# Gated-delta sample states as the moving operand in strips of 32 columns, and the convolution tails transposed one stage later

## The chip, the cores and the metric

The kernel runs on one core of a Trainium2 chip. The metric is the device time of one execution in microseconds (us). The engines named below are PE (TensorE, the matrix engine), DVE (VectorE), ACT (ScalarE), POOL (GpSimd) and SP (SyncE, which here only issues DMAs). PEld in a profile is PE's loading of stationary operands.

## The reference, cut to what matters

One inference step of a decoder trunk with four layers: retention, SSD (Mamba-2), gated DeltaNet (GDN below), retention, each followed by a squared-relu MLP. A prompt of 256 rows with empty past and a sample group of 8 sequences with 4 new rows each share the weights, so a matmul moves 288 rows. The change touches the sample group of GDN and the convolution state of SSD and GDN. The core of it, for the one chunk that the sample group has:

```
def step(S, inp):
    u_c, w_c, attn_c, qd_c, kd_c, cd_c = inp
    v_new = u_c - jnp.einsum('bhtk,bhkv->bhtv', w_c, S)
    o_c = jnp.einsum('bthk,bhkv->bthv', qd_c, S) + jnp.einsum('bhts,bhsv->bthv', attn_c, v_new)
    S = S * cd_c[..., None, None] + jnp.einsum('bshk,bhsv->bhkv', kd_c, v_new)
...
o = _rms(o, norm_w) * jax.nn.silu(z ...)
```

For each of 8 sequences b and 16 heads h there is a 128 x 128 state S. The step needs q·S and k·S for 4 rows each: 8 rows of 128 against every one of 128 states. Further, the last 3 rows ahead of each convolution go out as its new state (`new_buf`).

## The kernel before, in words

The dense products (`dense`, L195 to L224) go through PE as three fp32r matmuls for a k tile: ACT casts the weights to a high part (`wh`, L207), DVE takes the rest (`wl`, L210), and L222, L223 and L224 are the three products, each moving 288 columns. All else on PE is plain fp32; such a matmul of the program appears in the trace as two pairs of a weight load and a matmul, so eight in the program are x16 in a row of the trace.

A mixer runs its heads in four units, m = 0 to 3 (`units`). `weave` lets a unit's chain (its preparation, then its loop over chunks of the prompt) advance by one `yield`, and takes fillers for it: the gate's product, parts of the output product, and the projection of the next unit. The number that a chain yields is how much filler it wants (YS for SSD, YG for GDN), and the number of a filler is how much it counts. In GDN a side generator `sample(m)` is interleaved with the projection (`both`). The framework's scheduler then reorders each engine's instructions when the kernel is built, and each engine runs its queue in that order; buffers come from rotating pools, PSUM's small buffers in a pool with tag "m" (3) and tag "s" (2).

In GDN, a unit covers 4 heads. Its preparation makes decays (`ps_dif`), transposes of q and k (`ps_qk`, `ps_qs`), Gram matrices (`ps_gram`), then solves a triangular system: 15 steps on DVE (L1491 and L1492) followed by block products on PE (`ps_W`, `ps_Q`, from L1500 on), and, for the sample group, a small solve of its own (`ps_Y`, L1547 to L1565) that gives `Y2`, `vb2`, `at2` and the row scales `sc2`. The loop then runs over the prompt's chunks (`ps_vn`, `ps_S`, `ps_o`) and normalises (`on`).

`sample(m)` (L1572 to L1612) goes over two pairs of heads. For each head it loads the 8 states (`St`), and for each sequence makes one matmul with the state as the stationary operand and 8 columns of q and k as the moving one (`ps_kS`, 8 in the program for a head). ACT copies the result (`kS`, L1590), two matmuls with the identity transpose it (`ps_u`), DVE and ACT scale it (`r`, L1595; `qo`, L1597), then come `ps_n` with ACT's copy of it (L1601), `ps_o`, DVE's sum `o` (L1605), the square, the mean, POOL's inverse root (`rs_y`) and `on` (L1612), which `ps_oT` transposes for the output product. PSUM tiles of this generator have the tag "s".

`conv_state` (L836 on) transposes the convolution's tail rows (`tl`) through PE (`ps_cs`, PSUM tag "m"), copies them on ACT (`co`, L847) and issues DMAs for them; both mixers call it near the start of a unit's preparation.

Of the kernel before, what the change touches and what calls it, by code (L numbers as in the profile page):

```python
# [35 lines left out]
def make_consts():  # L36
# [87 lines left out]
class K:  # L124
# [808 lines left out]
    def ssd(self, ctx, j, i):  # L933
# [109 lines left out]
        def scan(m):  # L1043
            u = units[m]
            xs, Bt, Ct = u["xs"], u["B"], u["C"]
            hs = slice(8 * m, 8 * m + 8)
            self.conv_state(rp, u["tails"], O["p_ssd_conv"][j], O["s_ssd_conv"][j])

            xdt = rp.tile([128, 2, 512], F32, name="xdt", tag="xdt")
            xw = rp.tile([128, 2, 512], F32, name="xw", tag="xw")  # L1050
# [43 lines left out]
            for g in range(2):  # L1094
                ps = self.ps("ps_g")
                mm(ps[:, 160:416], Bt[g][:, 0:128], Ct[g][:, 0:256])
                mm(ps[:, 0:128], Bt[g][:, 128:256], Ct[g][:, 128:256])
                mm(ps[:, 128:160], rep2[:, 4 + g], Ct[g][:, SEQ:T])
                t = rp.tile([128, 416], F32, name="gm", tag=f"gm{g}")
                V.tensor_tensor(out=t, in0=ps[:, 0:416], in1=gmask, op=ALU.mult)  # L1100
                gm.append(t)
            yield YS[1]

            yi = self.ps("ps_yi")
# [139 lines left out]
    def gdn(self, ctx, j, i):  # L1244
# [109 lines left out]
        T64 = rp.tile([64, 8, 64], F32, name="T64")  # L1354
        G.memset(T64, 0.0)

        def proj(m):
            qk = rp.tile([128, 4, T], F32, name="qk", tag="qk", bufs=2)
            v = [rp.tile([128, T], F32, name="v", tag=f"v{a}") for a in range(4)]
            tails, tl = [], rp.tile([128, 8, 35], F32, name="tl", tag="tl", bufs=2)  # L1360
            for (c0, dst) in ((m * 256, [qk[:, 0], qk[:, 1]]), (1024 + m * 256, [qk[:, 2], qk[:, 3]]), (2048 + m * 512, v)):
                yield from self.conv_dense(rp, xh, xl, w[:, c0:c0 + len(dst) * 128], c0 // 128, rb, cw, cb, None, dst, tails, tl)
            units[m] = {"qk": qk, "v": v, "tails": tails}
# [7 lines left out]
        def prep(m):  # L1371
# [4 lines left out]
            for kh in range(2):  # L1376
                ps = self.ps("ps_dif", "s")
                h0 = 4 * m + 2 * kh
                for r in range(2):
                    mm(ps[:, r * 256:(r + 1) * 256], e2[:, h0 + r:h0 + r + 1].broadcast_to([128, 128]), cts)  # L1380
                Et = rp.tile([128, 2, 2, 128], F32, name="Et", tag=f"Et{kh}")
                pv = ps.rearrange("p (r t y) -> p r t y", r=2, t=2)
                for r in range(2):
                    for tt in range(2):
                        A.activation(Et[:, r, tt], pv[:, r, tt], AF.Abs, bias=nct[:, tt, h0 + r:h0 + r + 1])
                er = rp.tile([128, 2, 128], F32, name="er", tag="er")
                A.activation(er, pv[:, :, 1], AF.Exp)
                e_ = Et.rearrange("p r t y -> p (r t y)")
                A.activation(e_, e_, AF.Exp, scale=-1.0)
                G.tensor_tensor(out=qd[:, 2 * kh:2 * kh + 2], in0=er, in1=bcm(qk[:, kh, 128:256], 2), op=ALU.mult)  # L1390
                Es.append(Et)
            rb2 = rp.tile([128, 32], F32, name="rb2", tag="rb2")
            V.tensor_scalar(out=rb2, in0=i4, scalar1=g2[:, m:m + 1], scalar2=None, op0=ALU.mult)
            ps = self.ps("ps_dif2", "s")
# [2 lines left out]
            V.tensor_scalar(out=e1, in0=ps[:, 0:32], scalar1=gc[:, 32 + m:33 + m], scalar2=None, op0=ALU.subtract)  # L1397
            A.activation(e1, e1, AF.Abs)
            A.activation(e1, e1, AF.Exp, scale=-1.0)
            self.conv_state(rp, u["tails"], O["p_gdn_conv"][j], O["s_gdn_conv"][j], "on", 2)  # L1400

            ssq = rp.tile([128, 10], F32, name="ssq", tag="ssq", bufs=2)
            kt_ = kt("ktok", "vn", 1)
# [145 lines left out]
            def expand(k, t):  # L1549
# [16 lines left out]
            at2 = rp.tile([128, 128], F32, name="at2", tag="at2")  # L1566
            G.tensor_tensor(out=at2.rearrange("p (c y) -> p c y", c=4), in0=bcm(sm[:, 0], 4),
                            in1=b32.rearrange("p (c y) -> p c y", c=4), op=ALU.mult)
            u.update(Tm=Tm, L=L, at=Es, qd=qd, kd=kd, vb=vbs, ncf=ncf, eq=eq, sc2=sc2, Y2=Y2, x4=x4, vb2=vb2, at2=at2)

        def sample(m):
            u = units[m]  # L1572
            while "x4" not in u:
                yield None
            qk, Y2, x4, vb2, at2, sc2, eq = (u[n] for n in ("qk", "Y2", "x4", "vb2", "at2", "sc2", "eq"))
            on2 = u["on2"] = rp.tile([128, 128], F32, name="on2", tag="on2")
            for pr in range(2):
                hp = slice(64 * pr, 64 * pr + 64)

                pT = self.ps("ps_kS", "s")  # L1580
                pv = pT[:, 0:128].rearrange("p (h b c) -> p h b c", h=2, b=DB)
                for h in range(2):
                    St = rp.tile([128, DB, 128], F32, name="St", tag="St", bufs=3)
                    nc.sync.dma_start(St, I["state_gdn"][j, :, 4 * m + 2 * pr + h].rearrange("b k v -> k b v"))
                    for b in range(DB):
                        mm(pv[:, h, b], St[:, b], qk[:, pr:4:2, SEQ + b:T:DB])
                    yield 1.8
                kS = rp.tile([128, 2, 64], F32, name="kS", tag="kS", bufs=2)
                for a in range(2):
                    A.copy(kS[:, a].rearrange("p (h t b) -> p h b t", h=2, b=DB), pv[:, :, :, 4 * a:4 * a + 4])  # L1590
                pu = self.ps("ps_u2", "s")
                for a in range(2):
                    mm(pu[hp, a * 128:(a + 1) * 128], kS[:, a], ident)
                qo, r2, o2 = (rp.tile([128, 128], F32, name=n_, tag=n_) for n_ in ("qo", "r2", "o2"))
                V.scalar_tensor_tensor(out=r2[hp], in0=pu[hp, 128:256], scalar=sc2[hp, 2:3], in1=vb2[hp], op0=ALU.mult,  # L1595
                                       op1=ALU.add)
                A.activation(qo[hp], pu[hp, 0:128], AF.Copy, scale=eg2[hp, m:m + 1])  # L1597
                yield 1.0
                pn = self.ps("ps_n2", "s")
                mm(pn[hp, 0:128], Y2[hp, hp], r2[hp])  # L1600
                A.copy(x4[hp, 1], pn[hp, 0:128])  # L1601
                yield 1.0
                po = self.ps("ps_o2", "s")
                mm(po[hp, 0:128], at2[hp, hp], x4[hp, 1])
                V.tensor_tensor(out=o2[hp], in0=qo[hp], in1=po[hp, 0:128], op=ALU.add)  # L1605
                yield 1.0
                oo = rp.tile([128, 1], F32, name="oo1", tag="oo1", bufs=2)
                A.activation(qo[hp], o2[hp], AF.Square, accum_out=oo[hp])
                ms = rp.tile([128, 1], F32, name="ms1", tag="ms1", bufs=2)
                V.scalar_tensor_tensor(out=ms[hp], in0=oo[hp], scalar=1.0 / 128, in1=eq[hp, 4:5], op0=ALU.mult, op1=ALU.add)  # L1610
                r = self.rsqrt(ms, hp)
                A.activation(on2[hp], o2[hp], AF.Copy, scale=r[hp])  # L1612

        def loop(m):
            u = units[m]
# [212 lines left out]
```

## Time and profile before

| what | us |
| --- | --- |
| median of three runs | 2275.27 (2274.68 to 2281.68) |
| the profiled execution | 2272.98 |
| its span in the trace | 2271.1 |
| PE busy | 2186.3 |
| DVE busy | 1562.4 |
| ACT busy | 1243.3 |
| POOL busy | 580.0 |

The span starts with the first instruction that the trace holds. GDN's mixer stands at about 1060 to 1490 us of it, SSD's at about 520 to 860 us. The units of GDN begin with their first `ps_dif` at about 1122, 1218, 1310 and 1386 us. A row of the timeline gives the start, the duration, the engine and line, the output tile, the operands, and how often the instruction repeats back to back; a bracket at its end is the engine's idle time before it and what ended that.

### The profile page before, as it was taken

The numbers are of one execution on the slowest core, as the hardware profiler recorded it, in microseconds if no ns is written. First come the engines' busy times: TensorE is split into PE (matmuls) and PEld (weight loads), VectorE is DVE, ScalarE is ACT, GpSimd is POOL, SyncE is SP. The second block draws the span as 40 slices with busy tenths as digits, with TensorE's granted clock in tenths as the row PEclk, the third lists the DMA queues.
The fourth block names the chain that finished last, engine by engine and source line by source line (L and its number), as shares of the span: only waits on it lengthen the run. The fifth ranks groups of instructions, "written<-read, shape, count | busy, mean of one in ns | idle before, by whom it ended". The sixth has DMA issues, their size and how long they took to land. (4 is left out here: it accounts for less than half of the span.)

```text
span 2271.1 us, 43130 instructions
## 1 busy us (share of the span) xinstructions
PE 2186.3 (96%) x16332; PEld 2019.0 (89%) x16332; DVE 1562.4 (69%) x3211; ACT 1243.3 (55%) x2827; POOL 580.0 (26%) x605
## 2 busy tenths in 40 slices
PE   9999999998999999999898999989999999999998
PEld 7878899997889889999788987889999878889998
DVE  6777775557888877555886686466766677776554
ACT  4444455554767765545566566366644345445454
POOL 2100113332332222333322122034433001103333
PEclk9999999999999999999899999799999999999999
DMA  7876755545446545545443432257765666664553
GB/s 207 266 255 205 246 186 165 167 153 157 139 146 178 170 128 167 167 150 167 126 133 100 131 120 81 84 156 241 234 204 183 226 231 215 239 232 149 167 167 114
DMA packets 404076, 394.83 MB, mean 174 GB/s; under 512 B 12988, under 2 KB 353573, under 8 KB 403773
## 3 DMA queue, kind: packets, MB, share of 16 engines
q1 hardware_dynamic: 403708, 391.82, 54.3%
q8 instruction: 128, 2.10, 0.4%
q14 instruction: 80, 0.65, 0.1%
q10 hardware_dynamic: 96, 0.20, 0.0%
q0 software_dynamic: 64, 0.07, 0.0%
HBM read 333.36 MB, written 58.69 MB: 173 GB/s over the span
## 5 line engine op out<-in xcount | busy, mean ns | idle before, releaser
L207 ACT CAST wh<-raw 128x512 fp32r<-128x512 f32 x1024 | 627.8, 621 | 687.5 <-PE psd L223 642.5
L210 DVE TENSOR_TENSOR wl<-raw,wh 128x512 fp32r<-128x512 f32 x1024 | 744.3, 734 | 316.3 <-ACT wh L207 292.9
L222 PE MATMUL psd<-xh,wh 128*128 128x288 f32 x2576 | 775.4, 302 | 6.4 <-ACT xh L297 4.6
L224 PE MATMUL psd<-xh,wl 128*128 128x288 f32 x2576 | 771.6, 300 | 4.7 <-DVE wl L210 4.3
L223 PE MATMUL psd<-xl,wh 128*128 128x288 f32 x2576 | 771.0, 300 | 4.0 <-DVE xl L298 3.2
L222 PEld LDWEIGHTS psd<-xh,wh 128*128 128x128 f32 x2576 | 487.1, 189 | 25.1 <-issue 9.6
L223 PEld LDWEIGHTS psd<-xl,wh 128*128 128x128 f32 x2576 | 490.6, 190 | 17.6 <-issue 8.1
L224 PEld LDWEIGHTS psd<-xh,wl 128*128 128x128 f32 x2576 | 489.4, 190 | 13.4 <-DVE wl L210 7.6
L222 PE MATMUL psd<-ah,wh 128*128 128x288 f32 x1536 | 463.5, 302 | 10.0 <-DVE sg L543 3.7
L224 PE MATMUL psd<-ah,wl 128*128 128x288 f32 x1536 | 460.5, 300 | 4.1 <-DVE wl L210 4.0
L223 PE MATMUL psd<-al,wh 128*128 128x288 f32 x1536 | 461.6, 301 | 0.4 <-DVE al L465 0.4
L222 PEld LDWEIGHTS psd<-ah,wh 128*128 128x128 f32 x1536 | 293.9, 192 | 18.9 <-DVE x L442 4.2
L223 PEld LDWEIGHTS psd<-al,wh 128*128 128x128 f32 x1536 | 294.0, 191 | 9.6 <-issue 7.4
L224 PEld LDWEIGHTS psd<-ah,wl 128*128 128x128 f32 x1536 | 294.6, 192 | 7.6 <-DVE wl L210 5.5
L482 POOL TENSOR_TENSOR x<-x,dn 128x288 f32<-128x288 f32 x120 | 149.2, 1243 | 233.2 <-DVE dn L480 233.2
L463 POOL TENSOR_TENSOR a<-v 128x288 f32<-128x288 f32 x128 | 110.2, 861 | 271.9 <-ACT v L462 267.6
L726 DVE SCALAR_TENSOR_TENSOR S<-S,ps_up 128x512 f32<-128x512 f32 x128 | 83.5, 685 | 53.4 <-PE ps_up L725 50.7
L827 DVE SCALAR_TENSOR_TENSOR cacc<-U,cw,cacc 128x312 f32<-128x312 f32 x192 | 106.4, 561 | 8.2 <-ACT cacc L822 5.9
L465 DVE TENSOR_TENSOR al<-a,ah 128x288 fp32r<-128x288 f32 x128 | 59.0, 461 | 67.2 <-POOL a L463 66.5
L263 POOL TENSOR_TENSOR rs_y<-ms,mhalf 128x3 f32<-128x3 f32 (+3 forms) x37 | 36.7, 995 | 237.6 <-DVE ms L742 170.6
L803 POOL COPY U<-cb 128x24 f32<-128x24 f32 x64 | 34.1, 538 | 218.0 <-DVE cacc L827 120.5
L480 DVE TENSOR_TENSOR dn<-psd,rb 128x288 f32<-128x288 f32 x128 | 58.2, 455 | 40.0 <-PE psd L224 40.0
(504 smaller groups left out, 2651.7 us busy)
## 6 DMA issues: line engine op xcount, KB each, us to landing
raw<-mlp_w_up SPq DMA_DIRECT2D x64, 1024.0 KB
raw<-mlp_w_down SPq DMA_DIRECT2D x64, 1024.0 KB
raw<-ret_w_in SPq DMA_DIRECT2D x32, 1024.0 KB
S<-state_ret SPq DMA_DIRECT2D x64, 512.0 KB
s_ret<-S SPq DMA_DIRECT2D x64, 512.0 KB
raw<-ssd_w_in SPq DMA_DIRECT2D x24, 1024.0 KB
raw<-gdn_w_in SPq DMA_DIRECT2D x24, 1024.0 KB
raw<-ret_w_in SPq DMA_DIRECT2D x32, 512.0 KB
```

The source lines that it names most:

```text
L207: self.last_cast = nc.scalar.copy(wh, src)
L210: nc.vector.tensor_tensor(out=wl, in0=src, in1=wh, op=ALU.subtract)
L222: nc.tensor.matmul(po, lhsT=hs[k][:, os], rhs=xh[k], start=(k == 0), stop=False)
L223: nc.tensor.matmul(po, lhsT=hs[k][:, os], rhs=xl[k], start=False, stop=False)
L224: self.last_mm = nc.tensor.matmul(po, lhsT=ls[k][:, os], rhs=xh[k], start=False, stop=(k == kt - 1))
L263: self.nc.gpsimd.tensor_tensor(out=y[rows], in0=ms[rows], in1=self.mhalf[rows].broadcast_to([rows.stop - rows.start, n]), op=ALU.pow)
L463: nc.gpsimd.tensor_tensor(out=a, in0=v, in1=v, op=ALU.mult)
L465: nc.vector.tensor_tensor(out=al[o], in0=a, in1=ah[o], op=ALU.subtract)
L480: nc.vector.tensor_tensor(out=t, in0=ps, in1=rb2, op=ALU.mult)
L482: e.tensor_tensor(out=self.x[o], in0=self.x[o], in1=t, op=ALU.add)
L726: nc.vector.scalar_tensor_tensor(out=S[:, b, z], in0=S[:, b, z], scalar=C["g4"][h], in1=up, op0=ALU.mult, op1=ALU.add)
L827: nc.vector.scalar_tensor_tensor(out=acc[:, 0:n], in0=u, scalar=wk, in1=acc[:, 0:n], op0=ALU.mult, op1=ALU.add)
```

## The change

In `sample`, the states move and the queries and keys are stationary. POOL copies the 4 rows of q and of k of every sequence into a zero-padded tile `Z`, of which a window of 32 columns, chosen by the head, is a stationary operand; sequence b writes the strip of PSUM partitions that starts at 32·(b mod 4). Two sequences and two heads accumulate in a strip, so 16 matmuls, each moving 128 columns, fill one PSUM tile of 128 x 128, and the result is already transposed. The two matmuls of `ps_u` go, one ACT copy stands for two, and DVE's `r` and `o` and ACT's `qo` go. In their place the preparation makes `WQ`: two ACT scalings, two matmuls (`ps_wq`) with a new constant (`gdn_pm`, a permutation, 128 KB) and an ACT copy. `ps_n` and `ps_o` become two accumulating matmuls each. The square and `on` read `ps_o` straight from PSUM. `conv_state` is called after `ps_g` in SSD and after `ps_gram` in GDN. `er` lives in `qd` and has no tile of its own.

```diff
@@ SSD, preparation: the call of conv_state
-            self.conv_state(rp, u["tails"], O["p_ssd_conv"][j], O["s_ssd_conv"][j])
...
                 gm.append(t)
+            self.conv_state(rp, u["tails"], O["p_ssd_conv"][j], O["s_ssd_conv"][j])
             yield YS[1]
@@ GDN, preparation
+        Z = rp.tile([128, 2, DB, 40], F32, name="Z")
+        G.memset(Z, 0.0)
...
+            for pr in range(2):
+                for bh in range(2):
+                    bs = slice(4 * bh, 4 * bh + 4)
+                    G.tensor_copy(Z[:, pr, bs, 8:40].rearrange("p b (a x) -> p b a x", a=2)[:, :, :, bs],
+                                  qk[:, pr:4:2, SEQ:T].rearrange("p a (t b) -> p b a t", b=DB)[:, bs])
...
-            self.conv_state(rp, u["tails"], O["p_gdn_conv"][j], O["s_gdn_conv"][j], "on", 2)
...
                 mm(ps2[cs, 0:64], qk[:, 2 + q // 2, SEQ:T], qk[:, q // 2:4:2, SEQ:T])
+            self.conv_state(rp, u["tails"], O["p_gdn_conv"][j], O["s_gdn_conv"][j], "on", 2)
             yield YG[1]
...
+            t0, t1 = self.t128("wy"), self.t128("wq")
+            A.activation(t0, Y2, AF.Copy, scale=sc2[:, 2:3])
+            A.activation(t1, ident, AF.Copy, scale=eg2[:, m:m + 1])
+            WQ = rp.tile([128, 2, 128], F32, name="WQ", tag="WQ")
+            ps = self.ps("ps_wq", "s")
+            for a, t in enumerate((t0, t1)):
+                mm(ps[:, 128 * a:128 * a + 128], pm[:, a], t)
+            A.copy(WQ.rearrange("p a x -> p (a x)"), ps[:, 0:256])
@@ GDN, sample
                 pT = self.ps("ps_kS", "s")
-                pv = pT[:, 0:128].rearrange("p (h b c) -> p h b c", h=2, b=DB)
                 for h in range(2):
...
                     for b in range(DB):
-                        mm(pv[:, h, b], St[:, b], qk[:, pr:4:2, SEQ + b:T:DB])
-                    yield 1.8
-                kS = rp.tile([128, 2, 64], F32, name="kS", tag="kS", bufs=2)
-                for a in range(2):
-                    A.copy(kS[:, a].rearrange("p (h t b) -> p h b t", h=2, b=DB), pv[:, :, :, 4 * a:4 * a + 4])
-                pu = self.ps("ps_u2", "s")
-                for a in range(2):
-                    mm(pu[hp, a * 128:(a + 1) * 128], kS[:, a], ident)
-                qo, r2, o2 = (rp.tile([128, 128], F32, name=n_, tag=n_) for n_ in ("qo", "r2", "o2"))
-                V.scalar_tensor_tensor(out=r2[hp], in0=pu[hp, 128:256], scalar=sc2[hp, 2:3], in1=vb2[hp], op0=ALU.mult,
-                                       op1=ALU.add)
-                A.activation(qo[hp], pu[hp, 0:128], AF.Copy, scale=eg2[hp, m:m + 1])
+                        c = 32 * (b % 4)
+                        mm(pT[c:c + 32, 0:128], Z[:, pr, b, 8 - 8 * h:40 - 8 * h], St[:, b], h == 0 and b < 4, h == 1 and b > 3)
+                    yield 1.0
+                kS = rp.tile([128, 128], F32, name="kS", tag="kS", bufs=2)
+                A.copy(kS, pT[:, 0:128])
                 yield 1.0
                 pn = self.ps("ps_n2", "s")
-                mm(pn[hp, 0:128], Y2[hp, hp], r2[hp])
+                mm(pn[hp, 0:128], WQ[:, 0, hp], kS, True, False)
+                mm(pn[hp, 0:128], Y2[hp, hp], vb2[hp], False, True)
                 A.copy(x4[hp, 1], pn[hp, 0:128])
                 yield 1.0
                 po = self.ps("ps_o2", "s")
-                mm(po[hp, 0:128], at2[hp, hp], x4[hp, 1])
-                V.tensor_tensor(out=o2[hp], in0=qo[hp], in1=po[hp, 0:128], op=ALU.add)
+                mm(po[hp, 0:128], WQ[:, 1, hp], kS, True, False)
+                mm(po[hp, 0:128], at2[hp, hp], x4[hp, 1], False, True)
                 yield 1.0
...
-                A.activation(qo[hp], o2[hp], AF.Square, accum_out=oo[hp])
+                qo = self.t128("qo")
+                A.activation(qo[hp], po[hp, 0:128], AF.Square, accum_out=oo[hp])
...
-                A.activation(on2[hp], o2[hp], AF.Copy, scale=r[hp])
+                A.activation(on2[hp], po[hp, 0:128], AF.Copy, scale=r[hp])
```

Where the instructions then stand follows from the scheduler. On PE in unit m = 3, the second run of `ps_kS` in the queue of before (`psd` is a dense product, x8 in the program is x16 in the trace):

```order
L222 MATMUL psd<-ah_17880,wh 128x288
L223 MATMUL psd<-al_17884,wh 128x288
L1296 MATMUL ps_o_18703<-lkv,at_18439 64x128
L1296 MATMUL ps_kS<-qk,St 128x8 x16
L224 MATMUL psd<-ah_17880,wl 128x288
L222 MATMUL psd<-ah_17881,wh 128x288
L223 MATMUL psd<-al_17885,wh 128x288
L1296 MATMUL ps_u_18737<-c_ident,kS 64x128
```

And the same place now, up to the first block product of the solve (`ps_W`):

```order
L1302 MATMUL ps_kS<-St,Z 32x128 x15
L227 MATMUL psd<-ah_17874,wh 128x288
L228 MATMUL psd<-al_17878,wh 128x288
L229 MATMUL psd<-ah_17874,wl 128x288
L1302 MATMUL ps_n_18697<-kS,WQ 64x128
L1302 MATMUL ps_n_18697<-vb_18378,Y_18405 64x128
L1302 MATMUL ps_o_18701<-kS,WQ 64x128
L227 MATMUL psd<-ah_17875,wh 128x288
L228 MATMUL psd<-al_17879,wh 128x288
L1302 MATMUL ps_o_18701<-lkv,at_18436 64x128
L1302 MATMUL ps_kS<-St,Z 32x128 x8
L229 MATMUL psd<-ah_17875,wl 128x288
```

Before, both runs of 16 stood between the first `ps_Y` of m = 3 and that `ps_W`, with 96 dense matmuls; now 24 of the 32 stand there, with 70 dense ones, 8 follow behind the first 64 matmuls of `ps_W`, and the second `ps_n` and `ps_o` stand in the block products.

On PE at the start of the preparation of m = 0, before:

```order
L222 MATMUL psd<-xh_14198,wh 128x288 x2
L845 MATMUL ps_cs<-c_ident,tl 35x128 x3
L1296 MATMUL ps_dif<-cts,e_11537 128x256 x2
L223 MATMUL psd<-xl_14199,wh 128x288
L224 MATMUL psd<-xh_14198,wl 128x288
```

and now:

```order
L227 MATMUL psd<-xh_14202,wh 128x288 x2
L1423 MATMUL ps_qk<-c_ident,qk 128x128 x4
L1302 MATMUL ps_dif<-cts,e_11539 128x256 x2
L228 MATMUL psd<-xl_14203,wh 128x288
L229 MATMUL psd<-xh_14202,wl 128x288
```

Transposes of q and k have taken the place of those of the tails, which now follow `ps_gram`. On SP at the end of GDN (`u` and `St` are loads for the states' update that runs beside the MLP, `raw` are weights), before:

```order
L195 DMA raw<-gdn_w_out 128x4x512 x3
L195 DMA raw<-mlp_w_up 128x8x256
L1708 DMA p_gdn<-Sd 128x4x128
L1750 DMA u_19214<-gdn_u 128x256
L1755 DMA St<-state_gdn 128x8x128 x4
L195 DMA raw<-mlp_w_up 128x8x256 x3
```

and now:

```order
L1727 DMA p_gdn<-Sd 128x4x128
L1769 DMA u_19206<-gdn_u 128x256
L1774 DMA St<-state_gdn 128x8x128 x2
L200 DMA raw<-mlp_w_up 128x8x256
L1774 DMA St<-state_gdn 128x8x128 x2
```

The first load of the MLP's weights has moved behind the store of `p_gdn`, the load of `u` and two loads of states.

## Rows read from the trace of the kernel before

**Rows 1.** The page's first part: busy time, share of the span, instructions.

```profile
PE 2186.3 (96%) x16332; PEld 2019.0 (89%) x16332; DVE 1562.4 (69%) x3211; ACT 1243.3 (55%) x2827; POOL 580.0 (26%) x605
```

**Rows 2.** Busy time by stretch, with length, engines' busy time, granted clock, DMA share.

```profile
1130.00:1360.00 230.00, 215.71 (x1988) 199.17 (x1986) 176.00 (x474) 147.38 (x403) 57.39 (x79) 0.99 0.39 119
...
1426.00:1432.00 6.00, 6.00 (x28) 6.00 (x28) 1.62 (x6) 0.65 (x3) 0.00 (x0) 0.50 0.33 89
1434.00:1442.00 8.00, 8.00 (x58) 7.00 (x57) 7.12 (x27) 3.10 (x6) 0.00 (x0) 1.00 0.43 151
1444.00:1456.00 12.00, 12.00 (x46) 9.57 (x46) 4.01 (x12) 1.91 (x7) 0.00 (x0) 0.50 0.01 1
1458.00:1490.00 32.00, 25.93 (x301) 22.79 (x298) 12.38 (x30) 16.59 (x43) 4.93 (x7) 0.91 0.23 75
```

**Rows 3.** PE's timeline in unit m = 0, two groups of ps_kS among dense matmuls.

```profile
1168.49 1.84 PE L1296 MATMUL ps_kS<-qk,St 128*128 128x8 f32 x16
...
1170.40 0.29 PE L223 MATMUL psd<-xl,wh 128*128 128x288 f32 x1
...
1173.45 1.84 PE L1296 MATMUL ps_kS<-qk,St 128*128 128x8 f32 x16
```

**Rows 4.** PE's timeline around ps_qs: 32 stationary columns, 128 moving ones.

```profile
1140.89 0.29 PE L224 MATMUL psd<-xh,wl 128*128 128x288 f32 x1
1141.11 0.65 PE L1296 MATMUL ps_qs<-c_ident,qk 128*32 128x128 f32 x16
...
1141.92 0.29 PE L223 MATMUL psd<-xl,wh 128*128 128x288 f32 x1
```

**Rows 5.** PE's timeline around the two transposing matmuls of the sample group.

```profile
1178.32 0.29 PE L224 MATMUL psd<-xh,wl 128*128 128x288 f32 x1
1178.54 0.65 PE L1296 MATMUL ps_u<-c_ident,kS 128*64 128x128 f32 x4
...
1179.36 0.29 PE L223 MATMUL psd<-xl,wh 128*128 128x288 f32 x1
```

**Rows 6.** PE's timeline in unit m = 3, the two runs of ps_kS.

```profile
1423.60 4.71 PE L1296 MATMUL ps_kS<-qk,St 128*128 128x8 f32 x32
...
1441.20 5.38 PE L1296 MATMUL ps_kS<-qk,St 128*128 128x8 f32 x32
```

**Rows 7.** DVE's timeline in unit m = 3, the solve's steps and its longest waits.

```profile
1422.04 0.16 DVE L1491 TENSOR_TENSOR Ls<-Ls,X 128x15 f32<-128x15 f32 x1
...
1430.37 0.29 DVE L1565 TENSOR_TENSOR Y<-Y,ps_Y 128x128 f32<-128x128 f32 x1 [5.52 <-PE ps_Y L1296]
...
1447.11 0.69 DVE L210 TENSOR_TENSOR wl<-raw,wh 128x512 fp32r<-128x512 f32 x1 [5.22 <-PE psd L224]
...
1449.79 0.36 DVE L1595 SCALAR_TENSOR_TENSOR r<-ps_u,sc,vb 64x128 f32<-64x128 f32 x1 [1.84 <-PE ps_u L1296]
...
1455.03 0.46 DVE L442 TENSOR_TENSOR x<-x,psd 128x288 f32<-128x288 f32 x1 [2.94 <-PE psd L224]
...
1455.86 0.45 DVE L1499 STREAM_TRANSPOSE Ls<-Tm 128x256 f32<-128x256 f32 x1
```

**Rows 8.** PE's waits in GDN's stretch: total us, times, longest.

```profile
PE ps_dif L1296 <- DVE tl L813: 3.5, 1, 3.5
```

**Rows 9.** ACT's timeline at the end of unit m = 0.

```profile
1212.61 0.28 ACT L1590 COPY kS<-ps_kS 128x64 f32<-128x64 f32 x1 [0.77 <-PE ps_kS L1296]
...
1220.28 0.40 ACT L1612 ACTIVATE on<-o,rs_y 64x128 f32<-64x128 f32 x1 [0.77 <-POOL rs_y L263]
```

**Rows 10.** The timeline of all engines at the end of GDN.

```profile
1484.72 0.29 DVE L1605 TENSOR_TENSOR o<-qo,ps_o 64x128 f32<-64x128 f32 x1 [2.57 <-ACT on L1612]
...
1485.05 0.31 ACT L1608 ACTIVATE qo<-o 64x128 f32<-64x128 f32 x1 [0.36 <-DVE o L1605]
```

**Rows 11.** SP's timeline at the end of GDN: issues, with their duration.

```profile
1476.85 0.37 SPq L195 DMA_DIRECT2D raw<-mlp_w_up  x1
...
1490.86 4.17 SPq L1755 DMA_DIRECT2D St<-state_gdn  x4
```

More of the change, by code (lines that the diff above doesn't have):

```diff
@@ L110, in make_consts @@
     c["gdn_m4"] = np.stack([same & (jt[:, None] <= ut[None, :]), same & (ut[None, :] < jt[:, None])], axis=1).astype(f)
+    pm = np.zeros((128, 2, 128), f)
+    for a in range(2):
+        pm[x, a, 32 * (x % 4) + 16 * (1 - a) + 8 * (x // 32 % 2) + 4 * (x % 8 // 4) + x % 32 // 8] = 1.0
+    c["gdn_pm"] = pm
     u1 = np.zeros((128, 2, 128), f)
@@ L1257, in cload @@
             return t
-        b32, lms, gmask, m4, xi0, h16 = (cload(n) for n in ("gdn_b32", "gdn_lms", "gdn_gm", "gdn_m4", "gdn_x0", "gdn_h16"))
+        b32, lms, gmask, m4, xi0, h16, pm = (cload(n) for n in ("gdn_b32", "gdn_lms", "gdn_gm", "gdn_m4", "gdn_x0",
+                                                                "gdn_h16", "gdn_pm"))
         i4, s4 = m4[:, 0], m4[:, 1]
@@ L1385, in prep @@
                         A.activation(Et[:, r, tt], pv[:, r, tt], AF.Abs, bias=nct[:, tt, h0 + r:h0 + r + 1])
-                er = rp.tile([128, 2, 128], F32, name="er", tag="er")
+                er = qd[:, 2 * kh:2 * kh + 2]
                 A.activation(er, pv[:, :, 1], AF.Exp)
@@ L1389, in prep @@
                 A.activation(e_, e_, AF.Exp, scale=-1.0)
-                G.tensor_tensor(out=qd[:, 2 * kh:2 * kh + 2], in0=er, in1=bcm(qk[:, kh, 128:256], 2), op=ALU.mult)
+                G.tensor_tensor(out=er, in0=er, in1=bcm(qk[:, kh, 128:256], 2), op=ALU.mult)
                 Es.append(Et)
+            for pr in range(2):
[3 more added lines that the diff above has]
+                                  qk[:, pr:4:2, SEQ:T].rearrange("p a (t b) -> p b a t", b=DB)[:, bs])
             rb2 = rp.tile([128, 32], F32, name="rb2", tag="rb2")
@@ L1568, in prep @@
                             in1=b32.rearrange("p (c y) -> p c y", c=4), op=ALU.mult)
-            u.update(Tm=Tm, L=L, at=Es, qd=qd, kd=kd, vb=vbs, ncf=ncf, eq=eq, sc2=sc2, Y2=Y2, x4=x4, vb2=vb2, at2=at2)
+            t0, t1 = self.t128("wy"), self.t128("wq")
[6 more added lines that the diff above has]
+            A.copy(WQ.rearrange("p a x -> p (a x)"), ps[:, 0:256])
+            u.update(WQ=WQ, Tm=Tm, L=L, at=Es, qd=qd, kd=kd, vb=vbs, ncf=ncf, eq=eq, sc2=sc2, Y2=Y2, x4=x4, vb2=vb2, at2=at2)
         def sample(m):
@@ L1574, in sample @@
                 yield None
-            qk, Y2, x4, vb2, at2, sc2, eq = (u[n] for n in ("qk", "Y2", "x4", "vb2", "at2", "sc2", "eq"))
+            Y2, x4, vb2, at2, WQ, eq = (u[n] for n in ("Y2", "x4", "vb2", "at2", "WQ", "eq"))
             on2 = u["on2"] = rp.tile([128, 128], F32, name="on2", tag="on2")
```

## The prediction

> **What bounds the kernel now.** I read the shares of busy time first: PE is busy for 96% of the span and DVE for 69% [rows 1], so work taken off PE is worth something wherever DVE does not end the waits. A share over the whole span hides where that is, so the second view is the busy time by stretch, for GDN, the one mixer whose arithmetic changes. From 1130 to 1360 us, units m = 0 to 2 for the most part, PE is busy for 215.7 of 230 us and DVE for 176.0 [rows 2]: PE is the bound, but DVE follows at 77% and ends some of PE's waits. In unit m = 3 it is different. From 1426 to 1432 and from 1444 to 1456 us PE is busy without a gap while its granted clock is 0.50, which is 1.2 in place of 2.4 GHz, and DVE works only 1.6 of 6 and 4.0 of 12 us there [rows 2]. The timeline tells what PE did ahead of each fall: two runs of `ps_kS`, 4.71 and 5.38 us long, with nothing between their matmuls [rows 6]. While they run, the dense products that feed DVE stand behind them in PE's queue: DVE waits 5.52 us for `ps_Y` and 5.22 us for a dense product, and its solve stands still meanwhile [rows 7]. These runs are therefore both work and a block.
>
> **Units m = 0 to 2, by parts.** Between two groups of `ps_kS` 23 dense matmuls start in 1173.45 - 1170.40 = 3.05 us, 0.133 us each [rows 3]. A group (8 in the program, 16 in the trace) takes 1170.40 - 1168.49 = 1.91 us to the second dense start behind it; less one dense matmul that is 1.78 us, about 106 ns for each of the 16 with the change of shape aside [rows 3].
>
> No row shows the new form itself. The nearest is `ps_qs`, which has its very shape, 32 stationary columns in strips and 128 moving columns: from the dense start ahead of it to the second one behind it 1141.92 - 1140.89 = 1.03 us, less two dense matmuls 0.76 us for 16 [rows 4]. The upper bound is that nothing is gained, 1.78 us; the lower one that of `ps_qs`, since no row with that shape is faster. I take 0.76, because shape and operands' type agree, and what differs (it accumulates, and its states come by DMA) changes no count of columns. Twelve groups then save 12 x (1.78 - 0.76) = 12.2 us.
>
> The Trainium skill weighs against this on its page "TensorE: Matmul & The Clock Gate", section "Back-to-back issue gap", which has a sustained pace of about 81 ns per matmul with 128 moving columns and its own weight load. By that, 16 would take 1.30 us and the twelve groups save 5.8 us instead; the row's 0.65 us for 16 speaks against it [rows 4].
>
> The other parts. The two transposing matmuls of a pair of heads cost 1179.36 - 1178.32 - 0.27 = 0.77 us [rows 5] and are gone: 6 x 0.77 = -4.6 us. `ps_n` and `ps_o` have one matmul more each; with the same 0.58 us that the four records of `ps_u` take from 1178.54 on, that is +3.5 us for six pairs. `ps_wq`, two matmuls in a unit, is bounded by nothing and by a `ps_u` apiece; I take 0.77 us, +2.3 us for three units. The scheduler splits some groups among dense work; a change of shape costs 0.76 - 0.58 = 0.18 us, six more of them +1.1 us. The sum is -12.2 - 4.6 + 3.5 + 2.3 + 1.1 = -9.9 us of PE's time.
>
> Not all of it reaches the end, since DVE is busy for 77% and PE already waits 14.3 of 230 us [rows 2]. The same change frees DVE of a little: `r` at 0.36 us [rows 7] and `o` at 0.29 us [rows 10] for six pairs, 3.9 us of 176. I take three quarters, -7.4 us, between -2.5 (DVE ends most waits) and -9.9. ACT loses a copy and `qo` for each pair and gains three operations for each unit, POOL gains four small copies for each unit; neither engine is near its limit here (147.4 and 57.4 of 230 us [rows 2]), so these cost nothing as long as the copies do not stand ahead of an inverse root that is waited for.
>
> **Unit m = 3.** Before, the solve's steps begin at 1422.04 us and its last transpose at 1455.86 us, 33.8 us in all, of which DVE waited 5.52 + 5.22 + 1.84 + 2.94 = 15.5 us in four places [rows 7]. Without these it ends 18.3 us after its start. PE's work up to that point in the new order is 70 dense matmuls (9.3 us), three groups of `ps_kS` (2.3 us) and some ten small matmuls (about 2.5 us by [rows 5]), 14.1 us at the full clock, so DVE would set this stretch and up to 15.5 us would go. Of that something comes back: 30 dense matmuls (4.0 us), one group (0.8 us) and the second `ps_n` and `ps_o` (1.2 us) now stand behind the first `ps_W`, 6.0 us in a stretch where PE idles for 6.1 of 32 us [rows 2] but in a chain that waits for results. I let half of it show, +3 us, and take -12 us. If the clock still falls, 18 us at 0.50 cost 9 us again [rows 2], and only the shorter runs and little more is left, about -4; if all of it works, -15.
>
> **The tails, one stage later.** The count of transposes, copies and DMAs stays. What moves is the wait that PE has for a tail: in GDN 3.50 us once, at a `ps_dif` that stood behind three tail transposes [rows 8]; now transposes of q and k stand there, which need DVE as well, so most of the wait will find another name. I take -1 us, between 0 and -3.5. In SSD no wait of that size is shown and I take nothing, with 2 us to either side. SP's DMAs of the tails move with them, behind loads that nobody waits for.
>
> **The ends.** The last pair's chain loses DVE's `o`, 0.29 us, and the step to the square, 0.36 us [rows 10]: -0.65 us. `ps_o` now keeps its PSUM buffer until `on` has read it; with two buffers of that tag, the next pair's tiles share the other one. The first load of the MLP's weights was issued at 1476.85 us and now goes behind a load at about 1490.5 and two of four that took 4.17 us to issue, thus about 16 us later against the old clock [rows 11]. For both I add 2 us, between 0 and 7.
>
> **The sum.** -7.4 - 12 - 1 - 0.65 + 2 = -19 us. The profiled execution took 2272.98 us, and the median of the runs shown is 2.3 us above it; from the median the forecast is 2275.3 - 19 = 2256 us.
>
> **The rivals.** (A) DVE is the bound. Then units 0 to 2 give 2.5 instead of 7.4 us and m = 3 8 instead of 12: 2256 + 9 = 2265 us. For it speaks DVE's 77%, against it that the long waits in m = 3 are DVE's for PE [rows 7]. (B) The clock falls in m = 3 all the same, since PE then has less work and may stand idle for the solve: +8, 2264 us. Against it: between the two falls, from 1434 to 1442 us, with dense work, the clock was 1.00 [rows 2], and that is what the new order has there. (C) The strips do not overlap, and a group keeps its 1.78 us: three quarters of 12.2 come back, and 4 us in m = 3, 2256 + 13 = 2269 us, which is no change by the bound below. By the skill's pace it would be half of that, 2262 us.
>
> (D) Slower. The sample group's chain from `ps_kS` to `on` becomes what PE waits for. Before it took from 1212.61 to 1220.68 us, 8.1 us, at the end of m = 0 [rows 9], and dense work covered it. The new budgets give it less cover (`yield 1.0` for 1.8, and no `ps_u`), `ps_o` holds one of two PSUM buffers until the chain's end, and the next `ps_dif` needs one of them. If half of the chain, 4 us, lay bare for each of the eight pairs, that is +32, 2288 us; it is slower than before from about 3.3 us for a pair on, since eight of these are the 19 us of the gain and the 7 us of the bound below. Against it: POOL and ACT are half idle, and the same chain shows PE no long wait now. (E) Everything lands: -9.9 and -15 in full, -2 more for the tails, 2256 - 7.5 = 2248 us. That the change does not do what it says is excluded by the order of the instructions.
>
> **How the numbers follow.** The forecast has 0.50 (2250 to 2262), A 0.15, B 0.12, C 0.08, D 0.06, E 0.09. The range reaches from a little below E, which adds gains that no row bounds in SSD, to a little above C: 2246 to 2272 us; D and the tails of the others stay out. About 0.3%, 7 us, is what a measurement of this kernel can tell from no change, so faster means below 2268.4 and slower above 2282.1. Faster are the forecast, E, nearly all of A and B, and half of C: 0.82. Slower is D: 0.06. The rest, 0.12, is the same: half of C, the upper ends of A and B, and a milder D.
>
> **What would show each step right or wrong.** A group of `ps_kS` (x16, form 128*32 128x128) should take 0.65 us in the timeline; at 1.2 or more, C holds. No stretch of m = 3 between its `ps_Y` and its `ps_W` should have a granted clock near 0.50, and DVE should have no wait of 5 us there; the time from the first L1491 step to the last transpose should be near 18 to 22 us, not 33.8. If it is 22 or more with a full clock, DVE set it. PE's waits in GDN for ACT (`on`, `kS`, `x4`) should stay below some 5 us in all; 20 or more means D. The prediction would be wrong in size above all if PE's idle time in units 0 to 2 grows from 14 us by as much as its busy time falls, or if a gap appears in PE at the start of the MLP, where the weights' load now comes later.

## The result and the profile after

The changed kernel takes 2262.31 us in the median of four runs (2258.23 to 2265.39), the kernel before 2278.47 us beside it. The ratio is 0.993 with a 95% interval of 0.990 to 0.996, so it is faster by some 16 us (10 to 23). The forecast was 19. The sum was near, but two of its terms were far off in opposite directions, and the experiments say which.

The page's first part of the kernel after, the line that answers to [rows 1]:

```profile
PE 2175.3 (96%) x16348; PEld 1994.3 (88%) x16348; DVE 1562.1 (69%) x3195; ACT 1242.6 (55%) x2823; POOL 587.5 (26%) x622
```

The shares tell nothing. What tells is the time of a few landmarks on PE in both traces (us; "end" is the last `ps_oT` of GDN):

| | before | after | difference |
| --- | --- | --- | --- |
| first `ps_xt` of SSD | 585.4 | 584.7 | -0.7 |
| first `ps_gc` of GDN | 1112.6 | 1126.3 | +13.7 |
| first `ps_dif` of m = 0 to that of m = 3 | 264.6 | 256.1 | -8.5 |
| first `ps_dif` of m = 3 to the end | 102.3 | 84.7 | -17.5 |
| end to the end of the span | 782.5 | 780.2 | -2.3 |

From SSD's start to GDN's start the kernel after *loses* 14.4 us; GDN then wins 26. A group of `ps_kS` in PE's timeline of the kernel after, to be read against [rows 3] and [rows 4]:

```profile
1184.25 0.29 PE L229 MATMUL psd<-xh,wl 128*128 128x288 f32 x1
1184.47 0.64 PE L1302 MATMUL ps_kS<-St,Z 128*32 128x128 f32 x16
1185.05 0.40 PE L227 MATMUL psd<-xh,wh 128*128 128x288 f32 x1
1185.29 0.29 PE L228 MATMUL psd<-xl,wh 128*128 128x288 f32 x1
```

By the reckoning of the prediction that is 1185.29 - 1184.25 - 0.27 = 0.77 us, where 1.78 stood before. In m = 3, the busy time by stretch of the kernel after (columns as in [rows 2]); the cuts are the first `ps_dif`, the first `ps_Y`, the first `ps_W` behind the solve, and then the clock's fall:

```profile
1391.47:1419.49 28.02, 24.91 (x189) 22.80 (x189) 24.03 (x61) 17.91 (x47) 12.17 (x15) 0.94 0.21 70
1419.49:1434.81 15.32, 15.27 (x138) 12.62 (x136) 13.38 (x45) 6.94 (x17) 0.26 (x1) 1.00 0.48 160
1434.81:1440.00 5.19, 3.76 (x154) 2.88 (x154) 0.80 (x2) 4.04 (x13) 0.78 (x2) 0.94 0.48 173
1440.00:1458.00 18.00, 18.00 (x136) 14.52 (x136) 3.06 (x7) 4.99 (x13) 0.00 (x0) 0.50 0.01 2
1458.00:1477.00 19.00, 17.39 (x129) 16.52 (x128) 8.63 (x22) 9.49 (x22) 4.16 (x5) 0.95 0.21 70
```

and the same three parts before:

```profile
1386.39:1423.49 37.10, 31.81 (x244) 29.29 (x244) 25.85 (x68) 23.27 (x60) 14.65 (x18) 0.95 0.20 68
1423.49:1457.31 33.82, 33.82 (x183) 30.23 (x182) 15.50 (x54) 7.71 (x21) 0.00 (x0) 0.70 0.24 79
1457.31:1488.58 31.27, 25.20 (x356) 22.03 (x355) 11.64 (x28) 16.43 (x43) 4.93 (x7) 0.93 0.24 77
```

From `ps_Y` to `ps_W` 33.8 us became 15.3, at a clock of 1.00 in place of 0.70, with DVE busy for 13.4 of 15.3 us: its long waits are gone. PE is busy for nearly all of these 15.3 us, so DVE alone does not set the stretch. The solve's first step and its last transpose after, on DVE, to be read against [rows 7]:

```profile
1417.31 0.17 DVE L1506 TENSOR_TENSOR Ls<-Ls,X 128x15 f32<-128x15 f32 x1
...
1433.32 0.45 DVE L1514 STREAM_TRANSPOSE Ls<-Tm 128x256 f32<-128x256 f32 x1
```

That is 16.0 us where 33.8 stood before. Behind `ps_W`, up to the last `ps_oT`, 31.3 us became 41.4 with the 18 us at 0.50. The half clock has not gone; it has moved behind the solve. PE's longest waits in GDN after:

```profile
PE psd L229 <- DVE wl L215: 9.2, 6, 2.5
PE ps_Y L1569 <- DVE T L1568: 3.1, 2, 1.7
PE ps_oT L1748 <- ACT on L1703: 2.6, 3, 1.2
PE ps_dif L1302 <- DVE tl L818: 2.5, 1, 2.5
PE ps_S L1302 <- ACT vn L1677: 1.9, 4, 0.6
PE ps_oT L1749 <- ACT on L1631: 1.5, 3, 0.6
```

None of these is a wait for a PSUM buffer that the sample group holds; its `on` (L1631) is waited for as data of `ps_oT`, 1.5 us in all.

The loss in SSD stands in no wait of that size. It is seen in the path from a unit's first `ps_xt` to its first `ps_yi`; in unit m = 3, PE's timeline before:

```profile
805.24 0.60 PE L1054 MATMUL ps_xt<-c_ident,xs 128*128 128x128 f32 x4
...
813.92 0.82 PE L998 MATMUL ps_g<-Ct,Bt 128*128 128x256 f32 x4
...
817.75 0.64 PE L1126 MATMUL ps_yi<-sT,cm 128*32 128x256 f32 x8
```

and after:

```profile
810.78 1.03 PE L1058 MATMUL ps_xt<-c_ident,xs 128*128 128x128 f32 x8
...
819.10 0.59 PE L1003 MATMUL ps_g<-Ct,Bt 128*128 128x256 f32 x2
...
821.51 0.38 PE L850 MATMUL ps_cs<-c_ident,tl 128*35 128x128 f32 x2
824.62 0.84 PE L850 MATMUL ps_cs<-c_ident,tl 128*35 128x128 f32 x6 [1.40 <-ACT co L852]
826.47 0.64 PE L1131 MATMUL ps_yi<-sT,cm 128*32 128x256 f32 x8
```

The path took 12.7, 12.3, 12.3 and 12.5 us in the four units before, and 14.7, 15.8, 16.5 and 15.7 after: 49.8 against 62.7, 12.9 us more.

### The profile page after: what moved, and what is told of

Read it like the earlier page. It is cut to its first block, busy times and chain, and to the rows that moved or that the text cites. A ratio compares the mean times of both kernels' runs of the same rounds, so it can differ in the third digit from the quotient of the medians.

```text
span 2256.4 us, 43194 instructions
## 1 busy us (share of the span) xinstructions
PE 2175.3 (96%) x16348; PEld 1994.3 (88%) x16348; DVE 1562.1 (69%) x3195; ACT 1242.6 (55%) x2823; POOL 587.5 (26%) x622
## 5 line engine op out<-in xcount | busy, mean ns | idle before, releaser
L227 PEld LDWEIGHTS psd<-xh,wh 128*128 128x128 f32 x2576 | 487.2, 189 | 25.6 <-issue 10.1
L227 PEld LDWEIGHTS psd<-ah,wh 128*128 128x128 f32 x1536 | 291.1, 190 | 15.7 <-ACT wh L212 4.9
L832 DVE SCALAR_TENSOR_TENSOR cacc<-U,cw,cacc 128x312 f32<-128x312 f32 x192 | 106.5, 561 | 13.8 <-ACT cacc L827 11.6
```

The costliest lines, as they stand in the source:

```text
L227: nc.tensor.matmul(po, lhsT=hs[k][:, os], rhs=xh[k], start=(k == 0), stop=False)
L832: nc.vector.scalar_tensor_tensor(out=acc[:, 0:n], in0=u, scalar=wk, in1=acc[:, 0:n], op0=ALU.mult, op1=ALU.add)
```

## The experiments

In the tables below, "SSD" is the time from its first `ps_xt` to GDN's first `ps_gc` (527.2 us before, 541.6 after), "m = 3" that from its first `ps_dif` to the end of GDN (102.3 and 84.7). Both are read from one trace of a kernel, the medians from all its runs.

**Which part costs, which gives.** Four kernels, each a call put back or a part alone.

```diff
 # ssd_back: the changed kernel, SSD's call at the start of a unit again
+            self.conv_state(rp, u["tails"], O["p_ssd_conv"][j], O["s_ssd_conv"][j])
             xdt = rp.tile([128, 2, 512], F32, name="xdt", tag="xdt")
...
-            self.conv_state(rp, u["tails"], O["p_ssd_conv"][j], O["s_ssd_conv"][j])
             yield YS[1]
 # gdn_back: the same for GDN's call; sample_only: both; tails_only: the kernel before with both calls late
```

> The changed kernel with one call put back: SSD transposes its convolution tails at the start of a unit, as before. In the two traces the changed kernel reaches GDN 13.7 us later (its first ps_gc at 1126.3 us, against 1112.6), and from there to the last ps_oT it is 26 us shorter. Theory: the call's move in SSD costs 10 to 14 us, since the tails' 4 DMAs a group now stand in SP's queue ahead of the loads of SSD's states. Then this kernel takes 2264 - 12 = about 2250 us, 0.987 to 0.990 of the kernel before, and its ps_gc comes near 1113 us. Rival: the two executions differ in SSD by chance; then it is where the changed kernel is, 0.991 to 0.995, and its ps_gc lies anywhere.

> The changed kernel with the other call put back: GDN transposes its tails at the start of a unit, as before, SSD late. Theory: the move in GDN is worth 0 to 3 us, so 0.993 to 0.995 of the kernel before, with ps_gc near 1126 us as in the changed kernel. Rival: late tails in GDN cost as much there as they seem to in SSD, 10 us; then 0.988 to 0.990.

> Both calls put back: only the sample group's new form is left. Theory (late SSD tails cost 12 us, late GDN tails give 0 to 3): 2250 to 2256 us, 0.988 to 0.991 of the kernel before. Rival (the tails do nothing, the two traces differ by chance in SSD): as the changed kernel, 0.991 to 0.995.

> The kernel before with both calls late and nothing else. Theory: +12 us in SSD, 0 to -3 in GDN: 2285 to 2290 us, 1.003 to 1.006 of the kernel before, ps_gc near 1126 us. Rival (no effect in SSD): 0.998 to 1.001.

| kernel | median us | ratio (95% interval) | SSD | m = 3 |
| --- | --- | --- | --- | --- |
| ssd_back | 2256.69 | 0.991 (0.988 to 0.993) | 529.7 | 75.9 |
| gdn_back | 2257.46 | 0.990 (0.988 to 0.992) | 540.5 | 74.9 |
| sample_only | 2243.68 | 0.985 (0.982 to 0.987) | 530.0 | 74.8 |
| tails_only | 2285.32 | 1.003 (1.001 to 1.004) | 541.9 | 99.9 |

The traces agree among themselves: with SSD's tails late SSD takes 540.5 to 543.5 us in four traces, with them early 527.2 to 532.0 in seven, so late tails cost 12 us there. `tails_only`, without the new form, has just the paths from `ps_xt` to `ps_yi` of the changed kernel (14.7, 15.8, 16.5, 15.7). `sample_only` is 35 us faster than the kernel before, which is more than expected: late tails take back half of what the new form gives.

By the medians, against `sample_only`, late tails cost 14 us in SSD alone (`gdn_back`), 13 us in GDN alone (`ssd_back`: 0.988 to 0.993 against 0.982 to 0.987) and 18 us together (the kernel after, 0.993 against 0.985). With the old form both together cost 5 us (`tails_only`). So the two do not simply add, and in `gdn_back` the rival came in, not the theory. `ssd_back` has its `ps_gc` where it was expected (1114.9 us) and yet misses its time, 0.991 for 0.987 to 0.990. The traces of the table don't show GDN's part: from `ps_gc` to the end 342.6 us with its tails late (`ssd_back`) and 342.4 without (`sample_only`). But that trace of `ssd_back` is of the fastest of its six runs, 2241.04 us; the others took 2253 to 2261. That is taken up below.

**Why late tails are dear in SSD.** Two suspects could be taken away, and a third place tried.

```diff
 # ssd_actq: the changed kernel; SSD's tail DMAs from ACT's queue
-            nc.sync.dma_start(pout[0, :, cs], co[0:3, 0:n * 128])
+            q.dma_start(pout[0, :, cs], co[0:3, 0:n * 128])
...
 # ssd_co3: gdn_back with three tiles of 256 columns for one of 512
-            self.conv_state(rp, u["tails"], O["p_ssd_conv"][j], O["s_ssd_conv"][j])
+            self.conv_state(rp, u["tails"], O["p_ssd_conv"][j], O["s_ssd_conv"][j], "co", 3, 2)
...
 # ssd_later: gdn_back with SSD's call behind ps_ps, at the unit's end
-            self.conv_state(rp, u["tails"], O["p_ssd_conv"][j], O["s_ssd_conv"][j])
             yield YS[1]
...
             nc.sync.dma_start(O["p_ssd"][j, 0, hs].rearrange("(q r) p n -> (r p) q n", r=2), pst)
+            self.conv_state(rp, u["tails"], O["p_ssd_conv"][j], O["s_ssd_conv"][j])
             yield YS[5]
```

> The changed kernel, with SSD's tails late as in it, but their 48 DMAs issued from ACT's queue in place of SP's. In the changed kernel the second load of a state in SSD's unit m = 1 is issued at 695.9 us, 12.8 us later than before, behind the tails and weights in SP's queue. Theory: SP's queue is what makes late tails cost 11 to 13 us in SSD. Then ps_gc comes back to 1113 to 1117 us and the kernel takes about 2250 us, 0.986 to 0.990. Rival: the cost is in the PE and ACT work itself (ps_cs waits for the one co buffer and for the Gram product's DVE work; the Gram results and the states' products come later), then ps_gc stays at 1124 to 1128 us and the time near the changed kernel's, 0.991 to 0.995; an issue costs ACT something, which would add to it.

> The new form, GDN's tails early, SSD's behind ps_g as in the changed kernel, but with three ACT tiles of 256 columns for them in place of one of 512 (four groups of two in a unit in place of three). In the changed kernel a tail's transposes wait up to 1.4 us for the one tile, and the unit's three groups of stores go out 5 us apart. Theory: the single tile holds PSUM buffers that ps_yi needs, and this is the larger part of the 12 us; ps_gc then comes at 1113 to 1119 us, 0.984 to 0.987. Rival: the place itself costs, whatever the tile: ps_gc at 1124 us or later, 0.989 to 0.992.

> The new form, GDN's tails early, and SSD's tails not behind ps_g but at the end of a unit, behind ps_ps. Theory: late tails are dear in SSD because they stand between ps_g and ps_yi, on the unit's chain, where PE, ACT and the PSUM buffers of tag m are wanted; at the end of the unit nobody waits for them. Then ps_gc is at 1113 to 1118 us and the kernel at 0.984 to 0.987 of the one before. Rival: any place but the start of the unit is dear, since only there PE idles anyway (2.7 us of waits at ps_cs before): ps_gc at 1125 us or later and 0.989 to 0.992, as with SSD's tails behind ps_g.

| kernel | median us | ratio (95% interval) | SSD | `ps_xt` to `ps_yi`, m = 0 to 3 |
| --- | --- | --- | --- | --- |
| ssd_actq | 2262.58 | 0.992 (0.990 to 0.994) | 540.2 | 14.7, 15.7, 14.4, 15.9 |
| ssd_co3 | 2254.28 | 0.989 (0.986 to 0.992) | 540.6 | 14.7, 15.4, 12.4, 16.1 |
| ssd_later | 2241.09 | 0.983 (0.981 to 0.986) | 530.0 | 11.8, 11.6, 11.7, 11.8 |

The start of GDN, PE's timeline of `ssd_actq`, of `ssd_co3` and of `ssd_later`, one row each:

```profile
1124.98 1.06 PE L1303 MATMUL ps_gc<-g,gk 128*128 128x16 f32 x8
```

```profile
1125.55 1.06 PE L1302 MATMUL ps_gc<-g,gk 128*128 128x16 f32 x8
```

```profile
1115.85 1.06 PE L1302 MATMUL ps_gc<-g,gk 128*128 128x16 f32 x8 [0.26 <-DVE g L1315]
```

SP's queue was my first theory, and it fell: without the tails in it SSD keeps 11 of its 12 us, and `ssd_later` leaves them in it at no cost. (The second load of a state in m = 1 did come earlier in `ssd_actq`, at 690.6 us for 695.9; what ACT pays for the 48 issues is not measured.) The single tile as the cause of the larger part fell too. What decides is the place. Behind `ps_ps` the tails cost SSD nothing, and the path from `ps_xt` to `ps_yi` is even 0.7 us shorter in a unit than with the tails at its start.

Shown is that the place between `ps_g` and `ps_yi` costs, not that every unit gets longer by just what its path does. In m = 0 of the kernel after the path is 2.0 us longer, and m = 1 still begins 72.3 us after m = 0, where it was 72.7 before; in `ssd_co3` the path of m = 2 is back at 12.4 us, and SSD has gained nothing. How the 12 us split among PE's in-order queue, the order that the scheduler then gives everything else, and PSUM buffers, these runs don't tell. `ssd_later` has the lowest median of all kernels here, though its interval overlaps that of `sample_only`.

**The clock behind the solve.** The kernel after once more, and `ssd_back` once more, each for its trace.

> The changed kernel once more, for its trace alone: in its first trace PE's granted clock was 0.50 from 1440 to 1458 us, in m = 3 behind the solve, and m = 3 took 84.7 us, where the three kernels with the new form and a call put back took 74.7 to 75.9 us at full clock there. Theory: the fall belongs to this kernel's order of instructions, with the solve's end at 1434.8 us and an idle PE at 1438 us, so it is there again and m = 3 takes 84 to 86 us. Rival: it comes by chance from execution to execution; then m = 3 may take 75 us and the time be near 2250 us.

> The changed kernel with SSD's tails early, once more, for its trace: its runs spread from 2241 to 2261 us, and the one traced, the fastest, had m = 3 of GDN at the full clock (75.9 us). GDN's part stands there as in the changed kernel, whose two traces both have the clock at 0.50 behind the solve of m = 3 (84.7 and 84.9 us). Theory: that fall comes with this order in most executions but not in all, so a run of 2252 us or more has m = 3 at 84 to 86 us. Rival: the spread comes from elsewhere, and m = 3 is at 75 to 77 us whatever the time.

The kernel after took 2265.59 us with m = 3 at 85.0 us, and `ssd_back` 2250.23 us with m = 3 at 84.3 us, where the trace of its run of 2241.04 us has 75.9. The busy time of that stretch in `ssd_back`, first trace:

```profile
1430.00:1448.00 18.00, 17.49 (x189) 15.15 (x187) 6.79 (x16) 9.59 (x23) 2.08 (x2) 1.00 0.01 3
```

and second trace:

```profile
1430.00:1448.00 18.00, 18.00 (x141) 14.78 (x141) 3.34 (x7) 5.48 (x15) 0.00 (x0) 0.54 0.01 3
```

It is the same program at the same place, and 189 matmuls against 141. Ahead of it PE's timeline is the same in both; first and second trace:

```profile
1427.34 0.64 PE L1302 MATMUL ps_kS<-St,Z 128*32 128x128 f32 x16
1429.44 0.29 PE L227 MATMUL psd<-ah,wh 128*128 128x288 f32 x1 [1.46 <-issue]
```

```profile
1427.79 0.64 PE L1302 MATMUL ps_kS<-St,Z 128*32 128x128 f32 x16
1429.96 0.29 PE L227 MATMUL psd<-ah,wh 128*128 128x288 f32 x1 [1.52 <-issue]
```

So the fall is not tied to this order for good, as the first theory had it. The second fits, though this run has the fall at 2250 us already, below the 2252 that it named. The fall makes 8 to 9 us of the spread. Its runs of 2252 us and more left no trace, but each run's mean granted clock is on record: 0.987 at 2241.04 us, 0.981 at 2250.23, 0.975 and 0.976 in the three runs of 2260 us and more; in the four of `sample_only` 0.982 to 0.984.

Of ten traces with the new form five have the fall behind the solve of m = 3 (both of the kernel after, `ssd_actq`, `ssd_co3`, the second of `ssd_back`) and five don't. Sorted by the place of GDN's tails, four of the five with late tails have it, and one of the five with early ones (`ssd_co3`). So the 13 us of late tails in GDN seem to come in good part by the clock; the traces are few, and how the place of these transposes bears on the clock is not shown.

**What m = 3 gained from.** Two kernels with the old form, in which the first run of `ps_kS` in m = 3 is cut into pieces among dense work, and one with the new form treated the same way.

```diff
 # m3_spread: the kernel before; m3_spread2 also yields 0.45 after every two matmuls; sample_spread: sample_only
-                rest = [self.both(side(m), rest[0])] if rest else [side(m)]
+                if rest:
+                    rest = [self.both(side(m), rest[0])]
+                else:
+                    rest, fill = [self.both(side(m), fill[1])], fill[:1]
```

> The kernel before, old form of ps_kS, but in m = 3 sample alternates with a part of the output product, and it yields after every two of its matmuls, so that the first run of 16 in m = 3 is cut into pieces of 2 and 6 with 12 dense matmuls between; the second run stays whole. PE has the same work. Theory: what m = 3 gains from the change (its first ps_dif to the last ps_oT takes 102.2 us before, 74.7 with the new form alone) is for the most part not the matmuls' own 6.4 us but the block that a run puts on DVE's solve and the half clock that goes with it. Then this kernel has no 5 us wait of DVE in the first half of m = 3 and gains about half of what is not the matmuls' own, 5 to 10 us: 0.996 to 0.998 of the kernel before. Rival: the time of the matmuls counts, wherever they stand: 0.999 to 1.001, and m = 3 stays at 100 us or more.

> The kernel before with one difference: in m = 3, sample alternates with a part of the output product, so that the first run of ps_kS there stands in pieces of 4, 4 and 8; the second run stays whole, units m = 0 to 2 are untouched and no arithmetic changes. In the kernel with smaller pieces m = 3 took 90.8 us instead of 102.2, though the whole gained nothing, as the units ahead of it lost 18 us, where pieces of two stand among their dense work. Theory: the block on DVE by the first run is worth 5 to 10 us by itself, so 0.996 to 0.998. Rival: the time comes back elsewhere, 0.999 to 1.001.

> The new form with both calls of the tails put back, and in m = 3 sample alternates with a part of the output product as in the other kernel. With the new form no run is long enough to block DVE, so the theory is: no more than 2 us either way against the same kernel without this, 0.983 to 0.987 of the kernel before. Rival: order still matters there, and m = 3 gets shorter than 72 us.

| kernel | median us | ratio (95% interval) | m = 0 to 2 | m = 3 | of it `ps_Y` to `ps_W` |
| --- | --- | --- | --- | --- | --- |
| m3_spread2 | 2280.54 | 1.001 (0.9995 to 1.002) | 282.9 | 90.8 | 30.2 |
| m3_spread | 2283.43 | 1.001 (0.999 to 1.003) | 264.4 | 103.1 | 33.8 |
| sample_spread | 2246.69 | 0.986 (0.984 to 0.987) | 258.5 | 74.9 | 17.1 |

`m3_spread` tells nothing of the block: two of its three pieces still stand ahead of the last `ps_Y`, and DVE waits 5.13 us for it, about as before. `m3_spread2` does take half of that wait (2.8 us left), and 3.6 us go from `ps_Y` to `ps_W`, but the fillers moved and its units m = 0 to 2 lost 18 us. So how much of the gain is the block on DVE, how much the clock and how much the matmuls' own time stays open. `m3_spread2` shows something else, by accident. One of its runs of 32 now stands in m = 0, among dense work and far from any solve:

```profile
1213.49 5.83 PE L1299 MATMUL ps_kS<-qk,St 128*128 128x8 f32 x32
```

and the stretches around it, busy time and clock:

```profile
1205.00:1213.00 8.00, 7.87 (x62) 6.97 (x61) 4.77 (x13) 4.84 (x16) 1.26 (x3) 1.00 0.46 110
1213.00:1219.00 6.00, 6.00 (x36) 5.70 (x34) 0.28 (x1) 2.03 (x7) 0.95 (x1) 0.65 0.74 245
1219.00:1231.00 12.00, 12.00 (x45) 9.60 (x46) 2.25 (x6) 3.73 (x12) 0.88 (x2) 0.50 0.17 48
```

Before, that place had the clock at full speed and no such run:

```profile
1205.00:1231.00 26.00, 24.92 (x196) 22.54 (x197) 15.07 (x35) 18.59 (x57) 4.99 (x7) 1.00 0.22 74
```

So the half clock can come with a run of 32 of the old form in m = 0 as in m = 3 [rows 6]. It need not: another run of 32 in the same trace, in m = 2, has the full clock around it.

```profile
1394.03 3.74 PE L1299 MATMUL ps_kS<-qk,St 128*128 128x8 f32 x32
```

```profile
1390.00:1410.00 20.00, 20.00 (x163) 18.21 (x163) 7.53 (x20) 9.45 (x28) 2.52 (x3) 1.00 0.38 119
```

`sample_spread` shows that with the new form this change of order does not matter: 0.986 against 0.985.

## Why the prediction was right, step by step

*The price of a group* was right: 0.77 us measured for 0.76 taken from `ps_qs` [rows 4]. Rival C is out. The Trainium skill's pace ("TensorE: Matmul & The Clock Gate", section "Back-to-back issue gap") would have made it 1.30 us, an estimate from its 81 ns for each of 16. By the 0.77 us measured, that pace does not hold for these strips side by side.

*Units m = 0 to 2* were right: -8.5 us in the kernel after, -7.4 forecast. Nine of the ten traces with the new form lie between -6.1 and -8.5; in the tenth, `ssd_actq`, it is +1.1, with the clock at 0.50 from 1364 to 1381 us, in m = 2. In the kernel after PE's busy time in these units fell from 250.0 to 243.1 us and its idle time from 14.7 to 13.0, so the loss to idle time that was feared did not come.

*Unit m = 3* was right in that the long waits went, and wrong in its sizes, -17.5 us for -12. From `ps_Y` to `ps_W` -18.5 us came for the 15.5 forecast: DVE's waits went, and the clock there is 1.00; no run has the one without the other. That DVE would set this stretch was not borne out, since PE is busy for all of it. The "+3" behind `ps_W` became +10.1 in the kernel after, because rival B came true in another place: the clock falls, behind the solve. And what stands ahead of `ps_Y` was costed at nothing and gave -9.1 (37.1 to 28.0 us). That is order and no price of the new form: 18 dense matmuls fewer stand there, and the `ps_vn`, `ps_S` and `ps_o` of the last step of m = 2, 32 matmuls, now stand ahead of the first `ps_dif` of m = 3; `tails_only`, with the old form, has the same 28.0 us, and `sample_only`, with early tails, 29.1. Against `tails_only`, which differs from the kernel after by the new form and what comes with it in GDN, that form is worth -8.2 us in units 0 to 2, nothing ahead of `ps_Y`, -13.3 from there to `ps_W` and -1.9 behind.

In traces without the fall m = 3 gives 26 to 28 us. Summed over m = 3, the share of the clock not granted, times the time, is 14.3 us before, 1.7 in `sample_only` and 11.9 in the kernel after. So of the 27.5 us in `sample_only` the clock is 12.6 at most; in the two traces of `ssd_back` 11.9 us of that sum made m = 3 longer by 8.3.

*The tails* were the wrong step. "In SSD no wait of that size is shown and I take nothing, with 2 us to either side": it is +12 us, six times the bound. I had looked at what the moved transposes left, a place where PE waits, and not at what they came to stand in, a unit's path from `ps_g` to `ps_yi`; from `ps_xt` to `ps_yi` each unit took 2.0 to 4.2 us longer. GDN's -1 us was wrong as well, for the same reason: the wait at `ps_dif` did fall as forecast, from 3.5 us [rows 8] to 2.5, but late tails there cost 13 us in the median (`ssd_back` against `sample_only`), which seems to come in good part by the fall of the clock behind the solve.

*The ends* cost nothing: from the last `ps_oT` to the span's end 780.2 us after, 782.5 before, and 779 to 785 in all fourteen traces. The later load of the MLP's weights is not seen, nor is the longer hold of PSUM; rival D did not come. PE's waits on ACT in GDN sum to 6 us, 1.5 of them for the sample group.

In the two profiled executions the differences of the first table sum to 13.7 - 8.5 - 17.5 - 2.3 = -14.6 us, where the forecast's terms made -19. It is near by luck in part: +13.7 up to GDN's start was not forecast, and against it stand 5.5 us more from m = 3, 1.1 more from units 0 to 2, and 3.6 from the ends, which gave -2.3 for the +1.35 that was taken. The medians show the luck plainly: the new form alone gave 35 us where its terms made 18, and the tails took back 18 where -1 was forecast.

## What to carry to other kernels

Where a small matrix meets a large one, let the large one move and put the small ones side by side in strips: it cost 36 ns for a matmul in place of 106, and it gave back the transposes too. When work is moved "out of the way", look at the path that it comes to stand in, not only at the wait that it leaves; the same transposes cost 12 us behind `ps_g` and nothing behind `ps_ps`. A change of several parts deserves one kernel for each part, and every part more than one run: here the kernels without the late tails (0.985, and 0.983 with SSD's at the unit's end) beat the whole change (0.993).

## What the runs showed of the hardware

The traces hold eight runs of 32 matmuls with 128 stationary and 8 moving columns, 3.6 to 5.8 us in which PE has no gap: two before, one each in `tails_only` and `m3_spread`, four in `m3_spread2`. In seven of them the granted clock fell from 1.00 to 0.50 during the run or within 1.5 us behind it, and where no further run followed the half clock outlived the run by 4 to 13 us of busy PE. In the eighth (1394.0 us in `m3_spread2`) it stayed at 1.00. The clock also falls where no such run stands, as behind the solve in the kernel after. And the same program, with the same pause of 1.5 us on PE ahead of the same matmuls, kept the full clock in one execution and went at 0.54 of it for 18 us in another.
